# Gate rows stored from ScalarE, down sums moved, a row of its own for the last gate tile, head scaling on ScalarE, token blocks by column halves

## The chip, the core and the metric

The kernel runs on one core of one Trainium2 chip. A core has five engines that run side by side, each with an in-order queue of instructions: PE (TensorE, matrix products), DVE (VectorE), ACT (ScalarE), POOL (GpSimd) and SP (SyncE). DMA transfers are issued from the queues of SP, ACT and POOL and carried out by 16 DMA engines. An instruction that waits for something holds back all that stands behind it on its queue. Two memories on the chip matter here: SBUF, which holds tiles of 128 partitions, and PSUM, into which PE writes and which ACT and DVE read out.

The metric is the device time of one execution, in microseconds (us), the median of several runs.

## What is computed

One layer of a decoder trunk over 1024 tokens with 16 learned tokens ahead of them, D_MODEL 1024, in float32. A mixing block (a gated linear attention, "GLA", beside an "mLSTM") and then a convolutional feed-forward block. Cut to what the change touches:

```python
proj = h @ w_in + b_in.astype(h.dtype)
(g_q, g_k, g_v, g_r, g_lr, m_q, m_k, m_v, m_o, m_i, m_f, gate_a, gate_b) = jnp.split(proj, splits, axis=-1)
...
o_gla = from_chunks(head_rms(o_gla, gla_norm)) * jax.nn.silu(g_r)
...
o_ml = from_chunks(head_rms(o_ml, ml_norm.reshape(ML_H, 1, ML_DV))) * jax.nn.sigmoid(m_o)
y = jax.nn.sigmoid(gate_a) * (o_gla @ w_branch_gla) + jax.nn.sigmoid(gate_b) * (o_ml @ w_branch_ml)
return y @ w_out
```

`head_rms` scales each row of a head's output by its inverse root mean square. The feed-forward block is `(silu(gate) * up) @ w_down` with D_FF = 2816, after a causal convolution of width 3.

## The kernel before, in words

Channels lie on the partitions and tokens along the free dimension, in rows of 1040 (16 learned tokens and 1024). Every float32 operand of a product is split into a high part H, rounded for the matrix engine, and the rest L; a product is the sum of H*H, L*H and H*L, so three matmuls stand for one.

The stages, in order of time. Tiles are taken from pools; a tile with a tag shares its place with others of the same tag, and the first write to a reused place waits for the last use of the tile that had it.

*Heads* (to about 650 us). Four GLA heads (s = 0 to 3) and four mLSTM heads (s = 4 to 7). PE's main stream is the projections of the next head; the steps of the current head are a Python generator advanced between them. A head ends in `post` (L543): its output tiles `o(c)`, 128 tokens by 256 values for eight blocks, and `om` for the learned tokens, are scaled on POOL by a column of inverse norms (L548, L549), then transposed by PE (L558, tile "ot"; L564, "otm") and stored to DRAM (`osc`). The column itself is made on POOL as a power of -0.5 (L93). The three bare yields between put other work of PE's stream ahead of the transposes. After heads 3 to 6 `token_sums` (L458) makes sums and differences of token blocks on POOL, held behind `scaled`, the scaling of `om`, and stores them to DRAM (`tsc`).

*Gates* (about 650 to 1000 us). Thirty-two channel tiles of 128 are computed by `h @ w_in`: eight each of g_r, m_o, gate_a and gate_b. Six of gate_b (j = 0 to 3, 6 and 7) go one at a time through `merge_gate_b` (L450): 72 matmuls, three copies out of PSUM by ACT (L452) into a tile "gb" of tag "gst" (one buffer), and a store to DRAM (`gsc`, queue gscb) from SP. The tiles j = 0 to 2 run beside the last head, j = 3 as cover while the token blocks are loaded, and j = 6 and 7 after the pairs (END, L1137). The other 26 are taken in 13 pairs q (L1114 to L1135), each pair by a scheme of seven block products in place of eight: token halves and channel halves are summed and subtracted beforehand, which needs the token blocks T1 to T4 (`token_blocks`, L1059, tiles TH and TL from `tsc`) and the weight sums of `gate_weights` (L1008). `piece` (L960) is one of the two halves of a pair; its products go into the rows u0 and u1 (tiles gu0, gu1) by ACT (L984) and DVE (L977, L985, L986, L991, L992). The write of e2 (L985) is the first write of the pair into u1's second half; u1 has one buffer and u0 two.

`gate_finish` (L1078) ends a pair one step into the next: for pairs 0 to 7 it loads the head output, multiplies by the gate, and stores (`otd`); for pairs 8 to 12 it stores the raw rows u0 and u1 to `gsc` from POOL (L1082).

*Down sums.* `half_sums` (L1092) prepares the weights of the last product: two loads, four subtractions of [128 x 256] and two stores, all issued by POOL on one row. There are 22. Three follow each of the pairs 8 to 11 and two pair 12, four are made after the first merge product, and four in the loop over bm.

*Branch merge* (about 1000 to 1194 us). `load_o` (L1151) loads eight rows of a branch's output, splitting each (ACT makes ogH, DVE ogL). `prod3` (L1170) multiplies them by a branch weight, 72 matmuls of 342 columns into a PSUM tile of two buffers; for bg (GLA), j = 0 and 1 take the rows in the order in which they arrive. Each result is multiplied on DVE (L1203) by the sigmoid (ACT, L1200) of a gate_a row loaded by `merge_tile` (L1190). Rows yg4 to yg7 share places with the down sums of this stage (tags Y4 to Y7). Then come bm (mLSTM) with the gate_b rows sb, the output projection, and the feed-forward block to the end.

Order on each queue: the program is written in Python order, and a scheduler with priorities (`hp`) then places instructions, so what stands behind what on SP, ACT, DVE and POOL isn't the order of the source. `tc.issue_after(x)` asks that what follows on x's engine be placed behind x.

Of the kernel before, what the change touches and what calls it, by code (L numbers as in the profile page):

```python
# [17 lines left out]
P = 128  # L18
# [3 lines left out]
T = NM + SEQ  # L22
NK = D // P
NP = SEQ + 2
# [21 lines left out]
def hybrid_kernel(ctx, tc, x, meta, norm_mix, w_in, b_in, gla_w_gate, gla_b_gate, gla_norm,  # L46
                  ml_conv_w, ml_conv_b, ml_norm, w_branch_gla, w_branch_ml, w_out, norm_ffn,
                  ffn_w_up, ffn_conv_w, ffn_conv_b, ffn_w_down, norm_final, out):
    nc = tc.nc
# [9 lines left out]
    def hp(n):  # L59

        return tc.high_priority(offset=max(1, min(n, tc.cur_priority - floor[0])))
# [4 lines left out]
    wp = wctx.enter_context(tc.tile_pool(name="wp", bufs=3))  # L66
# [83 lines left out]
    def proj_cm(u, thirds, base, evac, bank=None):  # L150

        wH, wL = U.get(u, 2 if u > 2 else 0)
        for t0, n in thirds:
            pt = bank(t0) if bank else ps.tile([P, 512], F32, name=f"pj{u}_{t0}", tag="pj", bufs=3)
            i = 0
            for k in range(NK):
                for a, b in ((wH, xH), (wH, xL), (wL, xH)):
                    nc.tensor.matmul(pt[:, :n], a[:, k, :], b[:, k, base + t0:base + t0 + n],
                                     start=(i == 0), stop=(i == 3 * NK - 1))
                    i += 1  # L160
            with hp(PRI_E):
                evac(pt[:, :n], t0, n)
            yield
# [53 lines left out]
    TAIL, COVER, END = (0, 1, 2), (3,), (6, 7)  # L217
# [144 lines left out]
    for i in range(5, NC + 1):  # L362
        last, _ = norm_x(i)
# [6 lines left out]
    def cc(i):  # L370
        return col[:, i:i + 1]
# [34 lines left out]
    gsc = {g: dram.tile([NK, P, NP], F32, name=f"gsc{g}") for g in "ab"}  # L406
# [40 lines left out]
        heads[s]["v"] = vt  # L447
        yield from proj_v(uv[s], bB, vt)

    def merge_gate_b(j, bank=None):  # L450
        st = wp.tile([P, T], F32, name=f"gb{j}", tag="gst", bufs=1)
        yield from proj_cm(ugb[j], TH_POST, T0, lambda p, t0, n: nc.scalar.activation(  # L452
            st[:, t0:t0 + n], p, AF.Copy), bank)
        nc.sync.dma_start(gsc["b"][j], st[:, :NP])

    tsc = dram.tile([4, 4, P, 514], F32, name="tsc")

# [85 lines left out]
    def post(s, o, om, sc, ncols):  # L543

        h = s % 4
        g = "g" if s < 4 else "m"
        for c in range(NC):
            nc.gpsimd.tensor_scalar(o(c), o(c), sc[:, c + 1:c + 2], None, OP.mult)  # L548
        scaled = nc.gpsimd.tensor_scalar(om, om, sc[:2, 0:1], None, OP.mult)  # L549
        yield  # L550
        yield
        yield
        for j in range(2):
            of = hd.tile([P, T], F32, name=f"of{s}_{j}", tag="r", bufs=2)
            for gi in range(2):
                tp = ps.tile([P, 4, P], F32, name=f"ot{s}_{j}_{gi}", tag="s", bufs=3)
                for i in range(4):
                    nc.tensor.transpose(tp[:, i, :], o(4 * gi + i)[:, j * P:(j + 1) * P], ident)  # L558
# [5 lines left out]
            nc.tensor.transpose(tp[:, 0, :2], om[:, j * P:(j + 1) * P], ident[:2, :2])  # L564
# [351 lines left out]
    def advance():  # L916
        step(closing)
        while side and not step(side):
            pass
# [77 lines left out]
    gs = gs_ctx.enter_context(tc.tile_pool(name="gs", bufs=1, side="right", reuse_waits="tile"))  # L997
# [7 lines left out]
    NG = len(GATES) // 2  # L1005
# [47 lines left out]
    def weights_step(q):  # L1053
        if q < NG:
            next(wsteps[q])

    TB = {}

    def token_blocks():  # L1059
        for i in (0, 2, 1, 3):  # L1060
            h, l = TB[i] = [gs.tile([P, 4, 514], F32R, name=f"T{p}{i}", tag=f"T{p}{i}") for p in "HL"]
            nc.sync.dma_start(l.bitcast(F32), tsc[i].rearrange("k p c -> p k c"))
        for c in (slice(0, W0), slice(W0, 514)):
            for i in (0, 2, 1, 3):
                h, l = (t[:, :, c] for t in TB[i])
                nc.scalar.activation(h, l.bitcast(F32), AF.Copy)
                nc.vector.tensor_tensor(l, l.bitcast(F32), h.bitcast(F32), OP.subtract)
# [8 lines left out]
    gu = {}  # L1076

    def gate_finish(q):  # L1078
        for i, u in enumerate(gu.pop(q)):
            _, c, f, g, j = GATES[2 * q + i]  # L1080
            if f is None:
                nc.gpsimd.dma_start(gsc[g][j], u[:, :NP])  # L1082
                continue
            o = gs.tile([P, T], F32, name=f"go{q}_{i}", tag="o", bufs=2)
# [7 lines left out]
    def half_sums(pool, tag, bufs=1):  # L1092
        m, c = half.pop(0)
        t = pool.tile([P, T], F32, name=f"ts{m}{c}", tag=tag, bufs=bufs)[:, :D].rearrange("p (i n) -> p i n", i=4)
        for k in range(2):
            nc.gpsimd.dma_start(t[:, 2 * k:2 * k + 2], w_dn[P * (2 * m + k):P * (2 * m + k + 1), :].rearrange(  # L1096
                "p (i n) -> p i n", i=2)[:, :, 256 * c:256 * c + 256])
        for o, a, b in ((0, 1, 0), (1, 3, 1), (3, 3, 0), (2, 2, 3)):
            nc.gpsimd.tensor_tensor(t[:, o], t[:, a], t[:, b], OP.subtract)  # L1099
        for i in range(2):  # L1100
            nc.gpsimd.dma_start(tdn[i][m][:, :, 256 * c:256 * c + 256], t[:, 2 * i:2 * i + 2])
# [10 lines left out]
    u2 = wp.tile([P, T], F32, name="gu2", tag="gst", bufs=1)[:, :2 * W0].rearrange("p (a b) -> p a b", b=W0)  # L1112
    behind_ = None
    for q in range(NG):  # L1114
        gu[q] = [gs.tile([P, T], F32, name=f"gu{i}{q}", tag=f"u{i}", bufs=2 - i) for i in range(2)]
        for p in range(2):
            g = piece(psG, f"g{q}", p, gu[q], u2, WP[q], gate_block)
            next(g)
            if p == 1:
                weights_step(q + 1)  # L1120
            next(g)
            if p == 1:
                weights_step(q + 1)
            if behind_:
                next(behind_)
            if p == 0:
                weights_step(q)
                if q:
                    gate_finish(q - 1)
                weights_step(q + 1)  # L1130
            next(g)
            behind_ = g
        if q >= NK:
            for _ in range(3 if q < NG - 1 else 2):
                half_sums(gs, "o", 2)  # L1135
    next(behind_)
    for j in END:  # L1137
        ugb[j] = u_cm(w_in, O_GB + P * j, f"gb{j}")
    gate_finish(NG - 1)
    for j in END:  # L1140
        main(merge_gate_b(j, gate_bank(f"pe{j}")))
    gs_ctx.close()


# [2 lines left out]
    r2 = r2_ctx.enter_context(tc.tile_pool(name="r2", bufs=1, side="right", reuse_waits="tile"))  # L1147
# [34 lines left out]
    def th(t):  # L1182
        return t[:, :NP].rearrange("p (a b) -> p a b", a=3)
# [12 lines left out]
    for j in range(NK):  # L1196
        y = yg[j]
        if j < NK - 1:
            merge_tile(j + 1)
        nc.scalar.activation(y, y, AF.Sigmoid, bias=cc(C_GA + j))  # L1200
        pt = prod3(ubg[j], og, j < 2, f"bg{j}")
        with hp(PRI_E):
            nc.vector.tensor_tensor(th(y), pt, th(y), OP.mult)  # L1203
# [14 lines left out]
    for j in range(NK):  # L1218
# [6 lines left out]
        pt = prod3(ubm[j], om_, j < 1, f"bm{j}")  # L1225
# [237 lines left out]
    def po_bank(n, t, tag):  # L1463
        return psF.tile([P, 512], F32, name=f"po{n}_{t}", tag=tag)


    for i, tiles in enumerate(([1, 5, 2, 6, 0], [3, 7, 4, 8])):
        for n in range(4):
# [13 lines left out]
            for it, t in enumerate(rest):  # L1482
                pt = po_bank(n, t, ("V1", "X1")[it % 2])
# [19 lines left out]
    for q in range(NJ):  # L1503
        for p in range(2):
            g = up_piece(q, p)
# [239 lines left out]
    i = FIRST  # L1745
    while i < len(seq):
        r, ph, m = seq[i]
        k = i % NP2
# [52 lines left out]
```

## Time and profile before

| | us |
|---|---|
| median of 3 runs | 1978.6 |
| lowest and highest | 1977.29, 1978.92 |
| profiled execution | 1980.9 |
| its span, first to last instruction | 1979.2 |
| mean granted clock of PE | 0.977 |
| PE busy | 1880.7 |
| ACT busy | 827.7 |
| POOL busy | 461.3 |

How to read the rows below. A row of waits has the waiting engine, tile and line, what it waited for, and then the total, the number of waits and the longest. A row of the order of time has the start, the duration, engine, line and operation with output <- input; in brackets stands the idle time of the engine before it and what ended that. A row of windows has the stretch, its length, the busy time (with the number of instructions) of PE, PE's weight loads, DVE, ACT and POOL, and then PE's granted clock, the busy share of the DMA engines and GB/s. SPq is SP's queue, POOLq POOL's. Names of tiles are the program's, without buffer numbers.

### The profile page before, as it was taken

The numbers are of one execution on the slowest core, as the hardware profiler recorded it, in microseconds if no ns is written. First come the engines' busy times: TensorE is split into PE (matmuls) and PEld (weight loads), VectorE is DVE, ScalarE is ACT, GpSimd is POOL, SyncE is SP. The second block draws the span as 40 slices with busy tenths as digits, with TensorE's granted clock in tenths as the row PEclk, the third lists the DMA queues.
The fourth block names the chain that finished last, engine by engine and source line by source line (L and its number), as shares of the span: only waits on it lengthen the run. The fifth ranks groups of instructions, "written<-read, shape, count | busy, mean of one in ns | idle before, by whom it ended". The sixth has DMA issues, their size and how long they took to land. (4 is left out here: it accounts for less than half of the span.)

```text
span 1979.2 us, 32666 instructions
## 1 busy us (share of the span) xinstructions
PE 1880.7 (95%) x13377; PEld 1795.7 (91%) x13377; DVE 1196.8 (60%) x1775; ACT 827.7 (42%) x1297; POOL 461.3 (23%) x487
## 2 busy tenths in 40 slices
PE   8999999999999999965889999999999999999998
PEld 8999889899999999965889999999999999987776
DVE  6555636564442565644233344688787878886776
ACT  5354444544343433311142123554443434354563
POOL 3103303324353010177340120012222222200000
PEclk8999999999999999988889999999999999999999
DMA  5111011042322766666593353333334333378794
GB/s 162 33 36 57 22 56 53 16 131 72 96 76 80 182 164 157 159 187 180 166 343 105 106 188 101 129 119 111 102 108 133 107 107 107 113 270 308 282 375 157
DMA packets 220480, 270.02 MB, mean 136 GB/s; under 512 B 13422, under 2 KB 172672, under 8 KB 220331
## 3 DMA queue, kind: packets, MB, share of 16 engines
q1 hardware_dynamic: 205403, 220.95, 35.3%
q0 software_dynamic: 13088, 45.14, 7.5%
q8 instruction: 105, 1.72, 0.4%
q10 hardware_dynamic: 1840, 1.85, 0.3%
q14 instruction: 44, 0.36, 0.1%
HBM read 198.33 MB, written 69.57 MB: 135 GB/s over the span
## 5 line engine op out<-in xcount | busy, mean ns | idle before, releaser
L1361 POOL TENSOR_TENSOR SB<-SA,rg 128x512 f32<-128x512 f32 x20 | 32.0, 1598 | 234.9 <-issue 114.4
L1099 POOL TENSOR_TENSOR ts<-ts 128x256 f32<-128x256 f32 x88 | 74.5, 857 | 39.3 <-DMA ts<-in_ffn_w_down_dram 37.2
L201 PE MATMUL pv<-wH_mv,xH 128*128 128x256 f32 x256 | 75.5, 295 | 0.1
L201 PE MATMUL pv<-wH_gv,xH 128*128 128x256 f32 x256 | 75.3, 294 | 0.0
L957 PE MATMUL Yg<-xH,gHSB 128*128 128x258 f32 (+1 forms) x104 | 32.2, 309 | 43.7 <-DVE gu L985 43.7
L1448 PE MATMUL po<-wH_wo,yH 128*128 128x256 f32 x256 | 72.6, 284 | 0.1
L201 PE MATMUL pv<-wH_mv,xL 128*128 128x256 f32 x256 | 72.5, 283 | 0.0
L201 PE MATMUL pv<-wL_mv,xH 128*128 128x256 f32 x256 | 72.5, 283 | 0.0
L1448 PE MATMUL po<-wL_wo,yH 128*128 128x256 f32 x256 | 72.0, 282 | 0.3 <-DVE wL_wo L107 0.3
L201 PE MATMUL pv<-wH_gv,xL 128*128 128x256 f32 x256 | 72.0, 281 | 0.0
L201 PE MATMUL pv<-wL_gv,xH 128*128 128x256 f32 x256 | 72.0, 281 | 0.0
L1448 PE MATMUL po<-wH_wo,yL 128*128 128x256 f32 x256 | 71.7, 281 | 0.0
L1178 PE MATMUL bg<-ogH,wH_bg 128*128 128x342 f32 x192 | 62.7, 327 | 9.5 <-ACT gb L452 9.5
L1396 DVE SCALAR_TENSOR_TENSOR cv<-u,fc,cv 128x1024 f32<-128x1024 f32 x44 | 65.3, 1484 | 0.4
L1343 POOL TENSOR_TENSOR A<-u2raw,A 128x512 fp32r<-128x512 f32 x20 | 44.0, 2199 | 92.2 <-ACT A L1342 92.2
L1178 PE MATMUL bg<-ogL,wH_bg 128*128 128x342 f32 x192 | 62.7, 326 | 0.0
L1178 PE MATMUL bg<-ogH,wL_bg 128*128 128x342 f32 x192 | 62.5, 326 | 0.0
L957 PEld LDWEIGHTS Yg<-xH,gHSB 128*128 128x128 f32 x104 | 21.7, 209 | 44.7 <-DVE gu L985 44.7
L1096 POOL DMA_DIRECT2D ts<-in_ffn_w_down_dram x44 | 31.8, 728 | 128.9 <-DVE yM L1233 103.5
L675 POOL TENSOR_TENSOR pk<-pk,kT 128x256 f32<-128x256 f32 (+1 forms) x24 | 29.1, 1217 | 140.4 <-ACT pk L673 140.4
L1178 PE MATMUL bm<-omH,wH_bm 128*128 128x342 f32 x192 | 61.4, 320 | 0.0
L1178 PE MATMUL bm<-omH,wL_bm 128*128 128x342 f32 x192 | 61.3, 319 | 0.0
(749 smaller groups left out, 7566.6 us busy)
## 6 DMA issues: line engine op xcount, KB each, us to landing
gw<-in_w_in_dram SPq DMA_DIRECT2D x26, 512.0 KB
ts<-in_ffn_w_down_dram POOLq DMA_DIRECT2D x44, 256.0 KB, 4.4
tdn<-ts POOLq DMA_DIRECT2D x44, 256.0 KB, 2.7
rg<-in_ffn_w_up_dram SPq DMA_DIRECT2D x22, 512.0 KB
ru<-in_ffn_w_up_dram SPq DMA_DIRECT2D x22, 512.0 KB
adr<-s SPq DMA_DIRECT2D x40, 256.0 KB
rd<-in_ffn_w_down_dram SPq DMA_DIRECT2D x20, 512.0 KB
do<-tdn SPq DMA_DIRECT2D x18, 512.0 KB
```

The source lines that it names most:

```text
L201: nc.tensor.matmul(pt[:, :DV], a[:, k, t0:t0 + P], b[:, k % 4, :], start=(i == 0), stop=(i == 3 * NK - 1))
L675: eng.tensor_tensor(e, e, k, OP.mult)
L957: nc.tensor.matmul(out[:, :n], x[:, k, :], y[:, k, :], start=start and k == 0 and j == 0, stop=stop and k == 3 and j == 2, skip_group_chec ...
L1096: nc.gpsimd.dma_start(t[:, 2 * k:2 * k + 2], w_dn[P * (2 * m + k):P * (2 * m + k + 1), :].rearrange("p (i n) -> p i n", i=2)[:, :, 256 * c ...
L1099: nc.gpsimd.tensor_tensor(t[:, o], t[:, a], t[:, b], OP.subtract)
L1178: nc.tensor.matmul(pt[:, i, :n], a[:, k, :], b[k][:, t0:t0 + n], start=(k == 0 and j == 0), stop=(k == NK - 1 and j == 2))
L1343: eng.tensor_tensor(l, src, h.bitcast(F32), OP.subtract)
L1361: late.tensor_tensor(sb[:, 0:4], sa[:, 0:4], rg[:, 0:4], OP.subtract)
L1396: nc.vector.scalar_tensor_tensor(y, u[:, j:SEQ + j], fc[:, j, jj:jj + 1], y, OP.mult, OP.add)
L1448: nc.tensor.matmul(pt[:, :DV], a, b[:, k % 4, :], start=(k == 0 and i == 0), stop=(k == NK - 1 and i == len(terms) - 1))
```

## The change

It has five parts.

1. `gate_finish` issues its raw-row stores from ACT in place of POOL, and `merge_gate_b` issues its store from ACT in place of SP.
2. Pairs 8 to 11 are followed by two half sums in place of three. After the merge product bg1 three follow and after bg3 two, in place of four after bg0, written as held behind the merged product; the loop over bm takes the seven that are left (four before). The number of half sums is the same.
3. The last gate tile gb7 gets a row of tag "u0" (two buffers, free of gate pairs by then) in place of the single "gst".
4. `post` scales on ACT in place of POOL; after head 3 five yields stand before the transposes in place of three.
5. `token_blocks` takes the places of the tiles first and loads each by two column halves, all first halves ahead of the second; the first two rows go0 of tag "o" are taken between.

```diff
     def merge_gate_b(j, bank=None, st=None):
+        if st is None:
+            st = wp.tile([P, T], F32, name=f"gb{j}", tag="gst", bufs=1)
...
-        nc.sync.dma_start(gsc["b"][j], st[:, :NP])
+        nc.scalar.dma_start(gsc["b"][j], st[:, :NP])
...
         for c in range(NC):
-            nc.gpsimd.tensor_scalar(o(c), o(c), sc[:, c + 1:c + 2], None, OP.mult)
-        scaled = nc.gpsimd.tensor_scalar(om, om, sc[:2, 0:1], None, OP.mult)
-        yield
-        yield
-        yield
+            nc.scalar.activation(o(c), o(c), AF.Copy, scale=sc[:, c + 1:c + 2])
+        scaled = nc.scalar.activation(om, om, AF.Copy, scale=sc[:2, 0:1])
+        for _ in range(3 if s != 3 else 5):
+            yield
...
     def token_blocks():
         for i in (0, 2, 1, 3):
-            h, l = TB[i] = [gs.tile([P, 4, 514], F32R, name=f"T{p}{i}", tag=f"T{p}{i}") for p in "HL"]
-            nc.sync.dma_start(l.bitcast(F32), tsc[i].rearrange("k p c -> p k c"))
+            if i == 1:
+                places()
+            TB[i] = [gs.tile([P, 4, 514], F32R, name=f"T{p}{i}", tag=f"T{p}{i}") for p in "HL"]
         for c in (slice(0, W0), slice(W0, 514)):
+            for i in (0, 2, 1, 3):
+                nc.sync.dma_start(TB[i][1][:, :, c].bitcast(F32), tsc[i].rearrange("k p c -> p k c")[:, :, c])
...
+    def places():
+
+        for i in range(2):
+            go[0, i] = row(f"go0_{i}", "o", 2)
...
             if f is None:
-                nc.gpsimd.dma_start(gsc[g][j], u[:, :NP])
+                nc.scalar.dma_start(gsc[g][j], u[:, :NP])
                 continue
...
         if q >= NK:
-            for _ in range(3 if q < NG - 1 else 2):
+            for _ in range(2):
                 half_sums(gs, "o", 2)
...
-    for j in END:
-        main(merge_gate_b(j, gate_bank(f"pe{j}")))
+    for i, j in enumerate(END):
+        main(merge_gate_b(j, gate_bank(f"pe{j}"), row(f"gb{j}", "u0", 2) if i else None))
...
         with hp(PRI_E):
-            nc.vector.tensor_tensor(th(y), pt, th(y), OP.mult)
-        if j == 0:
-            for i in range(4, 8):
-                half_sums(r2, f"Y{i}")
+            merged = nc.vector.tensor_tensor(th(y), pt, th(y), OP.mult)
+        if j in (1, 3):
+            with tc.issue_after(merged.ins):
+                for i in (5, 6, 7) if j == 1 else (6, 7):
+                    half_sums(r2, f"Y{i}")
```

`row(name, tag, bufs)` is a [128 x 1040] tile of the gate stage's pool.

More of the change, by code (lines that the diff above doesn't have):

```diff
@@ L448, in value_proj, with merge_gate_b @@
         yield from proj_v(uv[s], bB, vt)
-    def merge_gate_b(j, bank=None):
-        st = wp.tile([P, T], F32, name=f"gb{j}", tag="gst", bufs=1)
+    def merge_gate_b(j, bank=None, st=None):
+        if st is None:
+            st = wp.tile([P, T], F32, name=f"gb{j}", tag="gst", bufs=1)
         yield from proj_cm(ugb[j], TH_POST, T0, lambda p, t0, n: nc.scalar.activation(
             st[:, t0:t0 + n], p, AF.Copy), bank)
-        nc.sync.dma_start(gsc["b"][j], st[:, :NP])
+        nc.scalar.dma_start(gsc["b"][j], st[:, :NP])
     tsc = dram.tile([4, 4, P, 514], F32, name="tsc")
@@ L1074, in gate_block, with row @@
         return [t[:, k0:k0 + 4, c0:c0 + n] for t in (xH, xL)]
-    gu = {}
+    gu, go = {}, {}
+    def row(name, tag, bufs=1):
+        return gs.tile([P, T], F32, name=name, tag=tag, bufs=bufs)
+    def places():
+        for i in range(2):
+            go[0, i] = row(f"go0_{i}", "o", 2)
     def gate_finish(q):
@@ L1081, in gate_finish @@
             if f is None:
-                nc.gpsimd.dma_start(gsc[g][j], u[:, :NP])
+                nc.scalar.dma_start(gsc[g][j], u[:, :NP])
                 continue
-            o = gs.tile([P, T], F32, name=f"go{q}_{i}", tag="o", bufs=2)
+            o = go[q, i] if q == 0 else row(f"go{q}_{i}", "o", 2)
             nc.gpsimd.dma_start(o[:, :NP], osc[g][j])
@@ L1114, in hybrid_kernel @@
     for q in range(NG):
-        gu[q] = [gs.tile([P, T], F32, name=f"gu{i}{q}", tag=f"u{i}", bufs=2 - i) for i in range(2)]
+        gu[q] = [row(f"gu{i}{q}", f"u{i}", 2 - i) for i in range(2)]
         for p in range(2):
```

## The prediction

> **What bounds the kernel now.** I read the page first, then the waits of PE, then the stretch in which the longest of them lie. One thing sets the end, PE:
>
> ```profile
> span 1979.2 us, 32666 instructions
> PE 1880.7 (95%) x13377; PEld 1795.7 (91%) x13377; DVE 1196.8 (60%) x1775; ACT 827.7 (42%) x1297; POOL 461.3 (23%) x487
> PE Yg L957 <- DVE gu L985: 43.7, 5, 15.6
> PE bg L1178 <- ACT gb L452: 9.5, 1, 9.5
> PE ot L558 <- POOL or L548: 5.0, 4, 2.3
> PE sc L626 <- POOL pk L675: 2.9, 3, 1.6
> PE sc L626 <- DVE pk L676: 2.7, 2, 1.7
> PE otm L564 <- POOL om L549: 0.6, 1, 0.6
> DVE gu L985 <- DMA gsca<-gu: 49.0, 4, 15.8
> ```
>
> PE has 98 us without work, and 43.7 of them are one line: the gate products wait for DVE's e2 write (L985). The last row says what DVE waits for: the landing of the store of a gate row. The same wait in order of time, with POOL, which issues that store:
>
> ```profile
> 852.82 0.41 DVE L992 TENSOR_TENSOR gu<-Zg,gu 128x256 f32<-128x256 f32 x1
> 873.38 0.42 DVE L985 TENSOR_TENSOR gu<-Yg,gu 128x256 f32<-128x256 f32 x1 [15.85 <-DMA gsca<-gu]
> 967.48 0.42 DVE L985 TENSOR_TENSOR gu<-Yg,gu 128x256 f32<-128x256 f32 x1 [10.60 <-DMA gsca<-gu]
> 864.61 0.81 POOL L1099 TENSOR_TENSOR ts<-ts 128x256 f32<-128x256 f32 x1
> 865.28 0.64 POOL L1082 DMA_DIRECT2D gsca<-gu  x1
> 957.22 1.20 POOL L1082 DMA_DIRECT2D gsca<-gu  x2
> ```
>
> The rows of pair 8 are whole at 853.2 (852.82 + 0.41). POOL, busy with half sums, issues the store of u1 only at 865.3 or 866.4, and it lands at 873.4. Tile u1 has one buffer, so the next pair's first write to it waits. Some 12 us are POOL's queue and 8 us travel. The first (15.85) and the last (10.60) of the four are shown.
>
> ```profile
> 780.00:840.00 60.00, 60.00 (x505) 60.00 (x504) 37.70 (x64) 22.27 (x33) 6.42 (x12) 1.00 0.67 163
> 855.00:980.00 125.00, 81.23 (x608) 80.21 (x607) 46.00 (x66) 18.86 (x30) 78.93 (x109) 0.82 0.59 176
> ```
>
> Two windows (busy time and count of PE, PEld, DVE, ACT, POOL, then PE's granted clock) price it. Undisturbed, 505 matmuls take 60 us, 0.1188 each. The 608 of the second window would take 72.2, with 0.4 more for eleven wider ones at its end; they took 125. The loss is **52 us**: 43.8 idle and about 8.6 of low clock after the idle times.
>
> [...]
>
> **1. Stores on ACT, two half sums per pair.** The eight gsca and two gscb stores are issued by ACT; they no longer queue behind half sums. Each new issue stands on ACT behind the copies of its pair and waits for the pair's last DVE write (L992). Behind it on ACT stand the next pair's copies from PSUM (L984), for which DVE and so PE wait; but those need products that come later anyway, and ACT is 15% busy there (18.86 of 125).
>
> The price of what remains: issue at 853.3, landing, and L985 takes 0.42. PE had waited 15.6 until 873.8, so it was ready at 858.2, and any L985 start up to 857.8 is free. No store from ACT's queue is in this trace. The nearest rows are the stores of the same 513 KB from SP's queue, whose landing the next copy into the same tile awaits:
>
> ```profile
> 648.50 0.32 SPq L454 DMA_DIRECT2D gscb<-gb  x1
> 653.71 0.46 ACT L452 ACTIVATE gb<-pc 128x342 f32<-128x342 f32 x1 [4.57 <-DMA gscb<-gb]
> 645.00:660.00 15.00, 15.00 (x97) 14.80 (x97) 4.52 (x8) 3.60 (x7) 0.54 (x1) 1.00 0.84 173
> 993.02 0.32 SPq L454 DMA_DIRECT2D gscb<-gb  x1
> 1001.27 0.80 ACT L452 ACTIVATE gb<-pe 128x342 f32<-128x342 f32 x2 [5.43 <-DMA gscb<-gb]
> 1005.00:1010.00 5.00, 0.14 (x1) 0.15 (x1) 2.69 (x3) 2.54 (x4) 3.29 (x5) 0.50 1.02 411
> gsca<-gu POOLq DMA_DIRECT2D x8, 513.0 KB, 8.1
> ```
>
> From issue to landing that is 5.2 us (653.71 - 648.50) at a share of the DMA engines of 0.84, and 8.3 (1001.27 - 993.02) where they are full (1.02 in the window from 1005). The stores from POOL took 8.1 (median, last row). The gate stage has a share of 0.59, so the first pair of rows is the nearest: landing at 858.5, 0.7 us late. With some ACT work in front of the issue (1 us) I take 1.25 for each of four pairs: **5 us remain**. Bounds: 0, and 4 x (853.3 + 8.3 - 857.8) = 15, with low clock up to 22. Gain 47, from 30 to 52.
>
> The half sums that leave the stage (14 become 10) are worked out under 3; inside the stage they free some 32 us of POOL (the time of four in the rows there), for which nobody then waits.
>
> **2. Scaling of heads on ACT.** 64 of L548 and eight of L549 leave POOL.
>
> ```profile
> L548 POOL TENSOR_SCALAR or<-or,rs3r 128x256 f32<-128x256 f32 x8 | 12.7, 1604 | 0.1
> L93 POOL TENSOR_TENSOR rs3r<-rs3v,mhalf 128x9 f32<-128x9 f32 x1 | 3.8, 3816 | 8.6 <-DVE rs3v L91 8.6
> L889 ACT ACTIVATE or<-op 128x256 f32<-128x256 f32 x32 | 12.2, 382 | 16.9 <-PE op L888 16.9
> ```
>
> The same shape takes ACT 0.38 us, so a head costs 8 x 0.38 + 0.4 (one for om) = 3.5 us of ACT instead of 7 to 13 of POOL. It removes PE's waits for L548 and L549, 5.0 + 0.6 = 5.6 us, all in head 3, where POOL's scaling takes 12.7. The two more yields for that head only put its transposes later. ACT has room: 8 x 3.5 = 28 on 828 of 1979. Behind each burst on ACT stand copies of the projection's sums; they come 3.5 us later at most, plus the wait for POOL's power (3.8 in head 3) if ACT gets there first. What hides that is the second PSUM buffer and PE's stream of projections. I take a gain of **5.6**; bounds: 11 (the waits of sc for pk, 2.9 + 2.7, go too) and a loss of 8.
>
> **3. End of the gates, branch merge.** Now the waits behind gb6 and gb7:
>
> ```profile
> 1007.46 1.06 ACT L1161 ACTIVATE ogH<-ogL 128x1026 fp32r<-128x1026 f32 x1 [2.47 <-DMA ogL<-otdg]
> 1009.86 0.65 PE L1178 MATMUL bg<-ogH,wH_bg 128*128 128x342 f32 x1 [9.49 <-ACT gb L452]
> 1024.20 1.23 DVE L1203 TENSOR_TENSOR yg<-bg,yg 128x1026 f32<-128x1026 f32 x1 [9.04 <-PE bg L1178]
> 989.91 2.85 POOL L1096 DMA_DIRECT2D ts<-in_ffn_w_down_dram  x4 [9.56 <-DMA gscb<-gu]
> 1021.16 0.68 POOL L1101 DMA_DIRECT2D tdn<-ts  x1 [0.30 <-POOL ts L1099]
> 980.53 2.38 SPq L1160 DMA_DIRECT2D ogL<-otdg  x4
> 1027.56 0.38 SPq L1160 DMA_DIRECT2D omL<-otdm  x1
> 1041.75 0.58 SPq L1160 DMA_DIRECT2D omL<-otdm  x1
> 1049.48 1.22 DVE L1203 TENSOR_TENSOR yg<-bg,yg 128x1026 f32<-128x1026 f32 x1
> ```
>
> gb7's copies waited for gb6's store; with its own row they don't, and the named 9.5 us go. But something else is late next. In the changed kernel's order SP issues, ahead of all eight ogL: a weight, the first sb (which waits for gb6's store), two omL (which wait for gb7's last matmul, 1009.86 - 9.49 = 1000.4) and the next weight (which waits for a split that needs gb7's weights released). So ogL leave at some 1004 and not from 980.53 on. The first ogH is then ready at 1011 to 1014, and bg0 takes its blocks in the pace of landings, 1.5 to 3.5 us each as the 2.47 shows. bg0 ends at 1025 to 1032 where it was 1024: a loss of 1 to 8, at best a gain of 2 (if loads land freely). I take 3.5.
>
> Then the five half sums that follow on POOL (Y5 to Y7 after bg1, Y6 and Y7 after bg3). Their hold by the merged product is not in the order of POOL's instructions; they begin when gb7's store frees the row, about 1006 to 1009. Before, four took 31.9 us (989.91 to 1021.84), five take 40. Behind the last stand yg7's load and six omL (14 us, 1027.56 to 1042.3), and the splits of omL stand ahead of the third merged product on DVE, which was at 1049.48 and would be at 1062 to 1070. PE needs that one's PSUM for bg4 at 1058 to 1064: 0 to 12, and I take **1**. Together **4.5 lost**. The seven in bm instead of four are 19 us more of POOL in a stage of 90 us; nothing waits for them before the down stage.
>
> **4. Token blocks by halves.**
>
> ```profile
> 649.54 10.30 SPq L1062 DMA_DIRECT2D TL<-tsc  x4
> 660.00:675.00 15.00, 12.18 (x93) 11.17 (x92) 10.67 (x10) 9.87 (x13) 0.00 (x0) 1.00 1.10 320
> PE Yg L957 <- DVE TL L1067: 0.9, 1, 0.9
> ```
>
> The four loads take 10.3 us on SP's queue since the third waits for a place; then PE starts the gates with idle time (2.8 in this window). With halves and the place taken before, it can go: gain **2.8**, bounds 0 and 2.8.
>
> **Sum:** 47 + 5.6 + 2.8 - 4.5 = 50.9. The profiled execution takes 1980.9 (span 1979.2 and 1.7 around it), 2.3 above the median of the runs, so 1930.0 there, and **1928** for the median of 1978.6.
>
> **Rivals.**
> - *A, the forecast*, 0.62: 1928, its own range 1918 to 1938.
> - *B, the merge stage pays much more*, 0.19: ogL land at 3.5 us each, 8 x 3.5 = 28 after 1011, so bg0 ends 15 late, and bg4's wait lies under that. For it speak full DMA engines (1.02) and the omL now ahead of them; against it the gaps of 1.5 seen too. 15 for 4.5: 1938.
> - *C, the change doesn't do what it says*, 0.12: the store's travel, not its place in a queue, is what DVE waits for. At 8.3 us from ACT as well, 15 to 22 remain for 5: 1938 to 1945, say 1941. For it: 8.1 of the 20 us from 853.2 to 873.4 were travel. Against it: 5.2 at a share of 0.84. [...]
> - *D, slower*, 0.04: ACT's bursts land on PE's path in every head. A burst is 3.5, with 3.8 before it for POOL's power: 7.3 x 8 = 58 more, 5.6 of gain gone: 1978.6 - 45.3 + 58 = 1991. It decides from 5.7 us a head on. Against it: ACT is 42% busy, and PE's waits in the heads name POOL and DVE.
> - The rest, 0.03: better than all that, down to 1914 (no remaining stall, heads 11, merge gains 2).
>
> B and C together would give 1951, so the range is **1915 to 1948**. A run tells about 0.2% (4 us) from no change: faster 0.94, same 0.02, slower 0.04.
>
> **What would show it.** 1: rows of L985 in pairs 9 to 12 with idle times below 3 us, clock 1.0 in the window after pair 8, and the last L992 some 47 us earlier. 2: no wait of ot for L548's successor, none larger of sc. 3: bg's first wait names ogH or ogL, and SP's ogL leave behind omL. 4: PE full between 660 and 675. Wrong would be: waits for gsca of over 4 us in each pair (C), or bg's waits above 15 us in sum (B).

## The result, and the profile after

| us | before | after |
|---|---|---|
| median | 1977.94 | 1960.26 |
| lowest to highest of 4 | 1975.61 to 1978.92 | 1959.70 to 1960.93 |
| profiled execution | 1980.9 | 1960.93 |

The ratio is 0.9912, with an interval of [0.9895, 0.993]: 17.7 us faster by the medians, 20.0 by the profiled executions. Forecast were 50.9: the sign came out, but 30.9 us of the gain, by the profiled executions, did not.

The span is 1959.2 us after, 1979.2 before. First the longest rows of the view of PE's waits (after; waiting tile, what it waited for, total, number, longest):

```profile
PE bg L1189 <- ACT ogH L1172: 15.8, 1, 15.8
PE bg L1189 <- DVE yg L1214: 11.2, 1, 11.2
PE po L1460 <- ACT hlo L1470: 6.3, 1, 6.3
PE Yg L957 <- DVE gu L985: 6.3, 5, 3.0
PE rtp L534 <- ACT of L560: 4.9, 1, 4.9
```

The 43.7 us of the gate rows have become 6.3. But bg, which waited 9.5 once, now waits 27.0 in two places, and two waits are new (rtp in head 3, po in the output projection).

Where in the execution that lies can be read without any idle time at all: the view of one line's instructions gives, for each group of matmuls, the start of the first and of the last. The last product of a stage is its end. After, then before:

```profile
L158 PE MATMUL pj<-xH,wH_gb x72: 313/318/508, 594.4 to 637.5; 128*128 128x342 f32 x72
L158 PE MATMUL pe<-xH,wH_gb x48: 313/318/430, 921.0 to 946.1; 128*128 128x342 f32 x48
L1189 PE MATMUL bg<-ogH,wL_bg x192: 313/320/487, 964.3 to 1070.9; 128*128 128x342 f32 x192
L1189 PE MATMUL bm<-omH,wL_bm x192: 313/319/325, 1071.4 to 1161.5; 128*128 128x342 f32 x192
L1460 PE MATMUL po<-wH_wo,yL x256: 277/282/415, 1161.9 to 1279.7; 128*128 128x256 f32 x128
```

```profile
L158 PE MATMUL pj<-xH,wH_gb x72: 313/318/509, 604.2 to 647.3; 128*128 128x342 f32 x72
L158 PE MATMUL pe<-xH,wH_gb x48: 313/318/425, 974.6 to 999.7; 128*128 128x342 f32 x48
L1178 PE MATMUL bg<-ogH,wL_bg x192: 312/320/488, 1010.6 to 1103.4; 128*128 128x342 f32 x192
L1178 PE MATMUL bm<-omH,wL_bm x192: 313/319/325, 1103.8 to 1194.0; 128*128 128x342 f32 x192
L1448 PE MATMUL po<-wH_wo,yL x256: 276/282/283, 1194.4 to 1299.9; 128*128 128x256 f32 x128
```

Differences of neighbouring ends give the length of each stage, beside what the prediction expected of it:

| stage (to the last ...) | before | after | gained | forecast |
|---|---|---|---|---|
| heads (gb2) | 647.3 | 637.5 | 9.8 | 5.6 |
| gates (gb7) | 352.4 | 308.6 | 43.8 | 49.8 |
| merge, GLA (bg7) | 103.7 | 124.8 | -21.1 | -4.5 |
| merge, mLSTM (bm7) | 90.6 | 90.6 | 0 | 0 |
| output projection (po) | 105.9 | 118.2 | -12.3 | 0 |

The feed-forward block differs by under 1 us. So 29 of the 31 us that are missing lie after the gates: 16.6 in the first merge product and 12.3 in the output projection. Both places follow, in order of time (after).

**The first merge product.** gb7's last matmul is over at 946.7.

```profile
946.76 0.81 SPq L1171 DMA_DIRECT2D omL<-otdm  x2
948.95 0.38 SPq L102 DMA_DIRECT2D wr_bg<-in_w_branch_gla_dram  x1
949.39 1.18 SPq L1203 DMA_DIRECT2D yg<-gsca  x1
950.74 9.68 SPq L1171 DMA_DIRECT2D ogL<-otdg  x8
960.11 1.15 ACT L1211 ACTIVATE yg<-yg,col 128x1026 f32<-128x1026 f32 x1 [5.89 <-DMA yg<-gsca]
961.39 1.06 ACT L1172 ACTIVATE ogH<-ogL 128x1026 fp32r<-128x1026 f32 x1
978.83 1.23 DVE L1214 TENSOR_TENSOR yg<-bg,yg 128x1026 f32<-128x1026 f32 x1 [1.62 <-PE bg L1189]
...
958.16 2.14 POOL L1107 DMA_DIRECT2D ts<-in_ffn_w_down_dram  x3 [50.14 <-DMA gscb<-gb]
998.90 0.68 POOL L1112 DMA_DIRECT2D tdn<-ts  x1 [0.30 <-POOL ts L1110]
1004.19 0.32 SPq L1203 DMA_DIRECT2D yg<-gsca  x1
1008.16 1.16 ACT L1211 ACTIVATE yg<-yg,col 128x1026 f32<-128x1026 f32 x1 [5.14 <-DMA yg<-gsca]
1009.23 1.04 ACT L106 ACTIVATE wH_bg<-wr_bg 128x1024 fp32r<-128x1024 f32 x1
1010.30 1.23 DVE L107 TENSOR_TENSOR wL_bg<-wr_bg,wH_bg 128x1024 fp32r<-128x1024 f32 x1 [19.70 <-ACT wH_bg L106]
1019.54 2.48 DVE L1173 TENSOR_TENSOR omL<-omL,omH 128x1026 fp32r<-128x1026 f32 x2 [1.94 <-ACT omH L1172]
1021.93 1.22 DVE L1214 TENSOR_TENSOR yg<-bg,yg 128x1026 f32<-128x1026 f32 x1
1023.30 0.63 PE L1189 MATMUL bg<-ogH,wH_bg 128*128 128x342 f32 x1 [11.25 <-DVE yg L1214]
```

Two losses. At bg0: SP has two omL, a weight and the first yg row ahead of the eight ogL; the omL wait for gb7's last matmul. The first split ogH runs on ACT at 961.39, behind the sigmoid of that yg row. The first merged product comes at 978.83, 32.1 after gb7's end; before, it came 23.8 after (1024.20 - 1000.4). That is 8.3. At bg4: POOL's half sums begin only when gb7's store has landed (958.16) and the last store leaves at 998.90. The row of yg7 shares its place, so its load leaves SP at 1004.19 and its sigmoid runs at 1008.16 on ACT, the high part of the next weight behind it at 1009.23, its low part on DVE at 1010.30, and then DVE splits six omL (the last two from 1019.54) before the merged product of bg2 at 1021.93. PE waits 11.2 for that one. The third merged product is 75.2 after gb7's end where it was 49.1 (1049.48 - 1000.4).

**The output projection.** PE's third new wait, in order of time (after):

```profile
1176.41 0.69 POOL L1112 DMA_DIRECT2D tdn<-ts  x1 [0.30 <-POOL ts L1110]
1179.06 0.34 SPq L1267 DMA_DIRECT2D h<-in_x_dram  x1
1179.56 0.68 SPq L102 DMA_DIRECT2D wr_wo<-in_w_out_dram  x1
1184.91 1.06 ACT L106 ACTIVATE wH_wo<-wr_wo 128x1024 fp32r<-128x1024 f32 x1 [6.18 <-DMA wr_wo<-in_w_out_dram]
1185.99 0.37 ACT L1470 ACTIVATE hlo<-po 2x256 f32<-2x256 f32 x1
```

The seventh half sum of the mLSTM stage uses the row Y6, and its last store leaves POOL at 1176.41. A row h of the output projection shares that place: its load stands on SP until 1179.06, the weights wr_wo stand behind it on SP, the split wH_wo waits for them on ACT (6.18), and hlo, which empties the PSUM bank that PE wants, stands behind that split. Four queues pass one late store on.

### The profile page after: what moved, and what is told of

The parts are those of the page before. It is cut to its first block, busy times and chain, and to the rows that moved or that the text cites. A ratio compares the mean times of both kernels' runs of the same rounds, so it can differ in the third digit from the quotient of the medians.

```text
span 1959.2 us, 32654 instructions
## 1 busy us (share of the span) xinstructions
PE 1876.5 (96%) x13377; PEld 1791.5 (91%) x13377; DVE 1187.0 (61%) x1775; ACT 857.1 (44%) x1369; POOL 372.8 (19%) x405
## 3 DMA queue, kind: packets, MB, share of 16 engines
q8 instruction: 105, 1.72, 0.4%
## 5 line engine op out<-in xcount | busy, mean ns | idle before, releaser
L1189 PE MATMUL bg<-ogH,wH_bg 128*128 128x342 f32 x192 | 63.3, 331 | 27.0 <-ACT ogH L1172 15.8
L1373 POOL TENSOR_TENSOR SB<-SA,rg 128x512 f32<-128x512 f32 x20 | 32.1, 1605 | 235.9 <-issue 114.1
L1189 PEld LDWEIGHTS bg<-ogH,wH_bg 128*128 128x128 f32 x192 | 37.7, 197 | 27.5 <-ACT ogH L1172 16.1
L1189 PE MATMUL bm<-omL,wH_bm 128*128 128x342 f32 x192 | 61.2, 319 | 0.0
```

Of the source, the lines that this page charges most:

```text
L1189: nc.tensor.matmul(pt[:, i, :n], a[:, k, :], b[k][:, t0:t0 + n], start=(k == 0 and j == 0), stop=(k == NK - 1 and j == 2))
L1373: late.tensor_tensor(sb[:, 0:4], sa[:, 0:4], rg[:, 0:4], OP.subtract)
```

## The experiments

The kernels ran on three chips, whose medians of the kernel before were 1977.8 (first four), 1972.2 (next four) and 1976.3 (last three), so ratios are compared; the changed kernel's is 0.9912. The stage lengths come from the same rows as above, in each kernel's profile, so each is that of one execution. Stages with the same code differ between executions: the gates take 300.4 in e6 and 309.1 in e10, whose edits differ only behind them, and the stages of the kernel before take 352.4 (gates) and 103.7 (GLA merge) in its profile, 344.0 and 99.7 in e8, which changes the heads alone. A difference in the gates of under 9 us, or in the merge of under 4, shows nothing by itself.

| | ratio to before, interval | median | gates | GLA merge | output proj. |
|---|---|---|---|---|---|
| e1 | 0.9831 [0.9811, 0.9852] | 1944.7 | 304.6 | 110.5 | 115.7 |
| e2 | 0.9859 [0.9835, 0.9883] | 1952.5 | 311.5 | 125.3 | 107.6 |
| e3 | 0.9900 [0.9885, 0.9915] | 1958.1 | 306.6 | 122.9 | 116.4 |
| e4 | 0.9812 [0.9787, 0.9838] | 1940.8 | 303.7 | 111.0 | 107.0 |
| e5 | 0.9856 [0.9829, 0.9882] | 1942.9 | 303.8 | 109.1 | 117.6 |
| e6 | 0.9817 [0.9796, 0.9839] | 1934.4 | 300.4 | 111.6 | 107.2 |
| e7 | 0.9880 [0.9855, 0.9905] | 1946.1 | 319.3 | 105.7 | 106.2 |
| e8 | 0.9966 [0.9947, 0.9985] | 1963.0 | 344.0 | 99.7 | 107.3 |
| e9 | 0.9794 [0.9772, 0.9815] | 1936.4 | 310.3 | 107.6 | 108.4 |
| e10 | 0.9781 [0.9766, 0.9796] | 1932.2 | 309.1 | 105.0 | 107.6 |
| e11 | 0.9770 [0.9740, 0.9801] | 1931.3 | 307.6 | 99.4 | 110.5 |

**e1: gb7 shares its row again.** The changed kernel without part 3.

```diff
-        main(merge_gate_b(j, gate_bank(f"pe{j}"), row(f"gb{j}", "u0", 2) if i else None))
+        main(merge_gate_b(j, gate_bank(f"pe{j}"), None))
```

> The changed kernel with part 3 alone undone: gb7 goes back to the one row of tag gst; its copies wait for gb6's store again. Theory (the own row is what the merge stage pays for: it moves the eight ogL loads behind omL and weights on SP, and it holds POOL's first half sum of the merge stage until gb7's store has landed): bg0's merged product about 24 us after gb7's last matmul (32 in the changed kernel, 24 before), POOL's first load of that stage some 25 us earlier than 958, PE's 11.2 us wait in bg gone, time 1940 (1935 to 1945). Rival (the five half sums and DVE's order of omL splits make the wait in bg, wherever POOL starts): bg0 is 8 earlier but the wait in bg grows by as much, time 1958 to 1961. Second rival (the own row is a gain of its 9.5 us, the rest lies elsewhere): slower, 1968.

The GLA merge is 14.3 us shorter, and the time at the upper end of the expected range. The view of its order of time:

```profile
922.95 3.58 SPq L1171 DMA_DIRECT2D ogL<-otdg  x5
925.45 1.44 POOL L1107 DMA_DIRECT2D ts<-in_ffn_w_down_dram  x2 [16.22 <-DMA gscb<-gu]
```

Five ogL leave 19 us before gb7's last product (942.2), and POOL's half sums start before it too (925.45), because the row that they wait for is released by the stores of pair 12 and not by gb7's. So the own row costs more than the 9.5 us that it takes away.

**e2: one half sum moved from the mLSTM merge into the gates.** Six where the changed kernel has seven.

```diff
-            for _ in range(2):
+            for _ in range(3 if q == NK else 2):
```

> The changed kernel with one half sum moved: three after pair 8, so that the loop over bm has six and not seven, and none lands on the row Y6 that h7's load needs next. Theory (the seventh half sum holds h7's load on SP until 1179, and the weights of the output projection stand behind it): PE's wait for hlo of 6.3 us goes, the output projection takes 106 us as before instead of 118, time 1948 (1946 to 1951). Rival (the output projection is slowed by the load of POOL, ACT and DMA at the end of bm): six for seven is worth 2 us, 1958. A cost in the gates, if POOL is at its limit there: L985's waits above 8 us in sum.

The wait for hlo is gone and the output projection is 10.6 shorter, back near before's 105.9. The seventh half sum is the cause of the third loss: in every experiment without it the output projection takes 106.2 to 110.5, in every one with it 115.7 or more. The gates are 2.9 longer, with 8.4 us of waits for L985 instead of 6.3, which is within what one execution differs from another. The median is 1.5 above the expected range.

**e3: DVE's splits of omL behind the merged product of bg2.** This takes the splits out of the way of the merged product for which PE waited.

```diff
+        prods.append(merged)
...
-    om_ = load_o("m", r1b, "R")
+    with tc.issue_after(prods[2].ins):
+        om_ = load_o("m", r1b, "R")
```

> The changed kernel with DVE's eight splits of omL queued behind the third merged product (bg2) and nothing else moved by hand; the half sums and yg7's load stay as late as they are. Theory (PE's 11.2 us wait in bg is DVE's order: the merged product of bg2 stands behind omL's splits, which wait for omL's loads behind yg7's): the wait goes, bg ends some 13 us earlier with the clock, time 1947 (1944 to 1951). Rival (yg7's late load itself sets it, through ACT, where wH_bg4 stands behind yg7's sigmoid): a wait for wL_bg of 5 to 11 us takes its place, time 1955 to 1961.

Only 1.9 us, no more than executions differ. bg still waits 9.6 us for yg, 8.8 of it at once. DVE in order of time:

```profile
1010.22 1.22 DVE L1215 TENSOR_TENSOR yg<-bg,yg 128x1026 f32<-128x1026 f32 x1
1021.52 9.18 DVE L1173 TENSOR_TENSOR omL<-omL,omH 128x1026 fp32r<-128x1026 f32 x8
1030.62 1.22 DVE L1215 TENSOR_TENSOR yg<-bg,yg 128x1026 f32<-128x1026 f32 x1
```

bg2's product is now early (1010.22), but all eight splits come in one piece before the next, and PE waits for that one. The wait moved by one product. As I had stated it, the theory fell: the place behind bg2's product only hands the wait on. The rival's time came (1958.1), but not the wait for wL_bg that it named. The place behind bg4's product is tried in e5 and e10.

**e4: the stores alone.** The kernel before, with one line of the change: the raw gate rows stored from ACT.

```diff
-                nc.gpsimd.dma_start(gsc[g][j], u[:, :NP])
+                nc.scalar.dma_start(gsc[g][j], u[:, :NP])
```

> The kernel before with one edit: the raw gate rows of pairs 8 to 12 are stored from ACT, not POOL; three half sums per pair stay, and all other parts of the change are left out. Theory (the place of the store in POOL's queue was the 44 to 47 us): L985's waits from 43.7 to 5 to 8 us, last gate matmul 42 to 47 earlier, and since the merge stage keeps its order, most of it arrives: 1936 (1930 to 1945). Rival (three half sums per pair can't be had without the stalls: POOL lags some 15 us behind and the merge stage's half sums, yg7 and omL come later): 1945 to 1955. Second rival (fewer half sums, not the queue, gave the gain): 1970 or more.

One edit gives 37 us by the medians, twice what the whole change gives. The gate stage is 48.7 shorter than in the profile before, and 40.3 shorter than in that of e8, whose gates have the code before. L985 waits 2.8 us in all, the longest 1.9, and the granted clock stays at 1.00 (window from 850 to 950 us). The GLA merge is 7.3 longer than before's: bg's waits are 10.9 (for gb) and 4.0 (for yg), and nothing waits for hlo.

**e5: the two orders by hand, everything else as changed.** On SP the loads of omL and sb go behind the last ogL; on DVE the splits of omL go behind the fifth merged product.

```diff
...
-    om_ = load_o("m", r1b, "R")
+    with tc.issue_after(loads[-1].ins), tc.issue_after(prods[4].ins):
+        om_ = load_o("m", r1b, "R")
...
-        nc.sync.dma_start(sb, gsc["b"][j])
+        with tc.issue_after(loads[NK - 1].ins):
+            nc.sync.dma_start(sb, gsc["b"][j])
```

> The changed kernel, gb7's own row and the five late half sums kept, but two orders set by hand: on SP the omL and sb loads behind the last ogL, on DVE the eight splits of omL behind the merged product of bg4 (the third run put them behind bg2's, and the wait went to bg5). Theory (the half sums that start late are the root; the orders on SP and DVE hand the delay on): bg0 up to 8 us earlier, but wH_bg4 still stands on ACT behind yg7's sigmoid, so bg4 can't start before about 65 us after gb7's last matmul; the stretch from there to bg's end falls from 125 to 111 to 114, time 1947 to 1950. Rival (the orders are the whole cost and the late half sums are harmless): the stretch falls to 104 as before the change, time 1940. Second rival (the wait only moves to another product again): 120 or more, 1956.

The GLA merge is 15.7 shorter with gb7's own row kept; the waits for yg fall from 11.2 to 2.0, the one for ogH from 15.8 to 11.2. The 109.1 lies between the theory's 111 to 114 and the rival's 104. And POOL's half sums are still late: their first load starts at 950.57, after 44.55 us of waiting for gb7's store. So the late half sums alone cost little (2.0 us of waits here); together with the splits ahead of bg2's product on DVE they cost more. The queue orders carry some 16 of the 21 us.

**e6: e1 and e2 together.**

> The changed kernel with gb7 back on the shared row and one half sum moved from bm to behind pair 8 (runs one and two together). If the two costs are separate, they add: 1944.7 - 8 to 10 = 1935 to 1937, bg's stretch 110, the output projection 107. If the eleventh half sum in the gates delays the merge stage's as much as it gains, 1943 or more with bg's stretch above 115.

The GLA merge (111.6) is close to that of e1, the output projection (107.2) that of e2: the two costs are separate. In the ratio it is 0.95% below the change (19 us), where the two stages say 14.3 + 10.6 = 24.9; its interval is 8 us wide. By the ratio the sum did not come in full: 1935 to 1937 on the first chip would be 0.979.

**e7: the change without parts 2 and 3.** Half sums and gb7 as before; stores, scaling and token blocks as changed.

```diff
...
-        if j in (1, 3):
-            with tc.issue_after(merged.ins):
-                for i in (5, 6, 7) if j == 1 else (6, 7):
-                    half_sums(r2, f"Y{i}")
+        if j == 0:
+            for i in range(4, 8):
+                half_sums(r2, f"Y{i}")
```

> The changed kernel without parts 2 and 3: stores on ACT, head scaling on ACT, token blocks by halves; half sums and gb7's row as before. Theory (parts 2 and 3 are what gave the gain back): 1940.8 of the run with the stores alone, less 6 for the heads and 3 for the token blocks: 1932 (1928 to 1936); bg's stretch 110, the output projection 107. Rival (parts 4 and 5 are worth nothing on top, the stages before the gates differ from run to run by as much): 1940.

A miss: 14 us above the 1932 expected, and 22 by the ratios, since this chip is the fastest of the three. By the ratios it is also 13 slower than e4. A wait that no other kernel has stands in the gates, 15.7 us of the last gate tiles (pe) for ACT's copy L453. POOL, SP and ACT in order of time:

```profile
940.38 0.68 POOL L1112 DMA_DIRECT2D tdn<-ts  x1 [0.30 <-POOL ts L1110]
943.06 2.70 SPq L1171 DMA_DIRECT2D ogL<-otdg  x5
949.41 1.06 ACT L1172 ACTIVATE ogH<-ogL 128x1026 fp32r<-128x1026 f32 x1 [19.50 <-DMA ogL<-otdg]
```

With three half sums a pair POOL lags; the first ogL leaves SP 2.7 us after a half sum's store at 940.38, which by these times is what it waits for. The split ogH stands on ACT ahead of gb6's last copy (951.32), so the gates' own products wait for a load of the next stage. e6 and e7 differ in the places of the half sums alone, and e6 is 11.7 us faster by the medians. The prediction gave part 2 no worth in the gates; beside the other parts it has one. e4 has three half sums a pair too and no such wait; it lacks parts 4 and 5 and the store of gb from ACT, and which of these makes the difference was not tried.

**e8: the scaling alone.** The kernel before with part 4 of the change.

> The kernel before with part 4 alone: the scaling of the heads on ACT and five yields after head 3. My step: the waits of ot and otm go and nothing new comes, 5.6 us: 1972 (1967 to 1976), last gate_b matmul of the heads' stage some 6 us earlier. Rival (ACT's bursts cost as much as they save): 1977 to 1982. If more than 8 us are gained, POOL's other work in the heads (pk) was held up by the scaling as well.

0.34% of 1972.2 is 6.7 us, 3 to 10 by the interval, for the 5.6 expected. But it isn't the expected 5.6. PE's waits for the scaled tiles are gone, and in their place, as in the changed kernel, stands the 4.9 of rtp. Windows of the second part of the GLA heads, in e8 and in e4 (which scales on POOL):

```profile
160.00:325.00 165.00, 162.60 (x1135) 151.94 (x1134) 100.16 (x166) 87.93 (x162) 23.51 (x24) 1.00 0.17 51
```

```profile
160.00:325.00 165.00, 159.76 (x1119) 149.36 (x1118) 97.67 (x162) 79.52 (x142) 41.65 (x42) 1.00 0.16 48
```

At the same clock PE is busy 2.8 us more of this stretch, with 18 us of POOL's work gone. The last GLA value projection starts at 316.1 in e8 and 320.1 in e4, the last matmul of gb2 at 637.8 and 643.6: 4.0 of the 5.8 us come before head 3's scaling. What is seen of waits there are those of sc for pk on POOL (2.9 before, 0.5 in the changed kernel); the rest of the 4.0 isn't assigned. That the gates and the GLA merge of e8 are 8.4 and 4.0 shorter than in the profile before is not shown to come from the scaling.

**e9: e5 and e2 together; e10: e6 with the splits of omL behind the fifth merged product.**

> The fifth run's orders with the second run's six half sums in bm; gb7's own row kept. If the three costs are separate (order on SP, order on DVE, h7's load), bg's stretch stays at 109 and the output projection falls from 118 to 107: ratio to the kernel before 0.980 (0.977 to 0.983). If the eleventh half sum in the gates delays the late half sums further, yg7's sigmoid holds wH_bg4 and bg's stretch grows to 114 or more: 0.983 to 0.986.

> The sixth run (gb7 on the shared row, six half sums in bm) with the splits of omL behind bg4's merged product on DVE. Theory (the 4.9 us wait for the merged product there is the same order on DVE): it goes, bg's stretch falls from 111.6 to 105 to 107, ratio 0.979 (0.977 to 0.982). Rival (yg7's sigmoid on ACT holds bg4 anyway): a wait of 3 to 5 for wL_bg in its place, ratio unchanged at 0.982.

In these two stages both come out as the sum of their parts: GLA merge 107.6 and 105.0, output projection 108.4 and 107.6. In e10 one order on DVE is all that differs from e6, and its 4.9 us wait for yg is gone. Two ways around the losses, with gb7's own row or without, end within each other's intervals.

**e11: the rows of the merge first.** e9, with two weights (bg3, bg4) and the first yg row behind the last ogL on SP, and the sigmoids of yg behind the last ogH on ACT.

```diff
-        nc.sync.dma_start(raw, src)
+        with tc.issue_after(loads[NK - 1].ins) if name in ("bg3", "bg4") else nullcontext():
+            nc.sync.dma_start(raw, src)
...
-    merge_tile(0)
     og = load_o("g", r2, "O")
+    with tc.issue_after(loads[-1].ins):
+        merge_tile(0)
...
-        nc.scalar.activation(y, y, AF.Sigmoid, bias=cc(C_GA + j))
+        with tc.issue_after(highs[NK - 1].ins):
+            nc.scalar.activation(y, y, AF.Sigmoid, bias=cc(C_GA + j))
```

> The ninth run, and the loads of ogL first of all in the merge stage: the weights of bg3 and bg4 and yg0 behind them on SP, yg0's sigmoid behind the ogH on ACT; gb7's own row is kept. Theory (what is left of the start is the place of the ogL in SP's queue): PE's first wait of bg falls from 11 to below 5, bg0's merged product comes 22 to 26 us after gb7's last matmul where it is 28 in the fifth run, bg's stretch 100 to 105, ratio 0.976 (0.973 to 0.979). Rival (it is the DMA engines, full there whatever the order): first wait 9 or more, ratio as in the ninth run.

SP in order of time (lines are a few lower in this kernel):

```profile
928.52 24.23 SPq L1175 DMA_DIRECT2D ogL<-otdg  x8
```

The ogL now leave from 928.52 on, seven of the eight before gb7's last matmul (which starts at 946.0), bg's first wait is 2.8 us, and the GLA merge takes 99.4: 25 less than in the changed kernel and as long as the 99.7 of e8 with the order before. POOL's half sums start late here too (953.12). It is 45 us faster than before (1976.3 to 1931.3) and, by the ratios, 28 faster than the change. By their intervals it and e10 can't be told apart.

## Why the prediction was wrong, and where it was right

**Step 1, the stores: right, and near in size.** Remaining waits of L985 behind pairs 8 to 11 were put at 5 us for four; the rows below, in order of time, show the longest of them, and 6.3 less the 1.06 of the first pair (in the last fence of this section) leaves 5.2. That the sum fits is in part luck: it was 1.25 for each, and one is 2.97. e4, the edit by itself, shortens the stage by 40 to 49, depending on which profile of these gates it is held against, for the 47 predicted. Rival C, that travel and not POOL's queue is the wait, is out.

```profile
863.58 0.33 ACTq L1093 DMA_DIRECT2D gsca<-gu  x1
871.62 0.42 DVE L985 TENSOR_TENSOR gu<-Yg,gu 128x256 f32<-128x256 f32 x1 [3.50 <-DMA gsca<-gu]
872.10 0.58 PE L957 MATMUL Yg<-xH,gHSB 128*128 128x258 f32 x1 [2.97 <-DVE gu L985]
```

and the window behind it:

```profile
873.00:877.00 4.00, 4.00 (x21) 4.00 (x21) 1.76 (x2) 0.00 (x0) 4.00 (x6) 0.50 0.60 153
```

What was off is one landing: 8.0 us from the issue at 863.58, close to the upper bound (8.3) and not the 5.2 chosen. The DMA engines were full there (a share of 1.12 from 863.6 to 871.6), so the row of the 8.3 was the nearest one, and not that of 5.2, chosen by the stage's mean share of 0.59. After PE's wait of 2.97 the clock is 0.50 for four us, where the 5 us of the prediction had no low clock in them; that is some 2 us. The low clock that its bound adds to 15 to make 22, some 7 us for four waits of 3.8, is a term that no run shows: what the changed kernel showed is these 2, behind one wait. In e2 and e10 the clock fell to 0.50 after shorter waits as well, of 1.72 to 1.94 (the last section has a row).

**Step 2, the scaling: right in size by luck, wrong in place and price.** The 5.6 of waits in head 3 went, and 4.9 came back as rtp's wait for ACT (L560); most of what was gained came from elsewhere. The price of the scaling on ACT was taken from a row of another form, too low:

```profile
L549 ACT ACTIVATE or<-or,rs3r 128x256 f32<-128x256 f32 x8 | 3.3, 496 | 3.7 <-POOL rs3r L93 3.7
```

496 ns and not 382, so a head costs 4.5 us of ACT and not 3.5. The gain came from the GLA heads before 325 us (e8). In the stage table the heads gain 9.8; e4, whose heads are before's own, ends them at 643.6, so 6.1 are the change's and 3.7 go with before's profiled execution, whose clock was 0.98 from 160 to 325 us where e4 had 1.00.

**Step 3, the merge: the step that failed first.** "4.5 lost" was made of 3.5 at bg0, from a range of 1 to 8, and of 1 at bg4, from 0 to 12. They measured 8.3 and 12.8 (21.1 less 8.3). The mechanism was told right, queue by queue; each value was taken below the middle of its own range, the second near its kind end, and the result is just above both unkind ends. At bg0, the first split ogH was put at 10.6 to 13.6 us after gb7's end (1011 to 1014 less 1000.4) and was ready 15.8 after: its load travels while the DMA engines are full (a share of 0.99 between 946.7 and 962.5). The sigmoid ahead of it on ACT adds little at most, since seven of the eight splits wait for their own loads (5.7 us in all). At bg4, the third merged product was put at 62 to 70 us after gb7's end (1062 to 1070 less 1000.4) and came 75.2 after. A link was left out of that chain: the sigmoid of yg7 also holds back the next weight's high part on ACT, for which DVE waits 19.7 us before it comes to the splits of omL. No run moves that sigmoid alone. Rival B gave this outcome 0.19 with 15 lost at bg0; the loss is larger and most of it is at bg4. B's own sign, waits of bg above 15 us in sum, is there with 27.0.

**The sentence that failed outright** is the last of step 3: the seven half sums in the mLSTM stage are "19 us more of POOL in a stage of 90 us; nothing waits for them before the down stage". It asked who reads the sums, not who takes their rows next. h does, and through SP and ACT that cost 12.3 (e2 gives 10.6 of them back). No rival had it, and with the merge's loss it carries the time out of the range.

**Step 4, the token blocks: nothing gained.** The idle times of 2.8 are there in the kernel after as well, under other names. Before, four waits for the blocks make 2.7, the longest 1.11. PE and ACT in order of time, after:

```profile
657.88 0.39 PE L957 MATMUL Xg<-TH,gHSB 128*128 128x258 f32 x1 [1.90 <-DVE gu L977]
664.51 1.06 ACT L1069 ACTIVATE TH<-TL 128x1024 fp32r<-128x1024 f32 x1 [3.47 <-DMA TL<-tsc]
666.35 0.39 PE L957 MATMUL Yg<-xH,gHSB 128*128 128x258 f32 x1 [1.06 <-DVE gu L985]
```

The 2.7 us of waits for the blocks are now 3.0 us of waits for DVE's rows. Both kernels split the blocks in eight pieces, on ACT and then on DVE, and behind these splits stand the pair's copies: ACT's last piece waits 3.47 for its load, the copy out of PSUM (L984) runs behind it at 665.47, DVE's L985 waits for that copy, and PE for L985. The blocks still come late; the wait for them has moved behind ACT and DVE. The bound of 0 was the right end; no run takes this part alone.

**The sum.** Of 30.9 us that the profiled execution falls short, 16.6 are the GLA merge, 12.3 the output projection and 6.0 the gates (2.8 the token blocks, 2 low clock, the rest not assigned), less 4.2 that the heads gave above the forecast; that leaves 0.2 for all else. Most of the 4.2 is the 3.7 of before's profiled execution (step 2).

## What to carry to other kernels

When work is moved to a later stage, ask of each buffer that it holds who takes that place next, and follow that taker through its queue: here one store late on POOL held a load on SP, the weights behind it, a split on ACT and at last PE. Where a term is the end of such a chain, and other work is queued on its links, take the middle or the unkind end of its range unless every link's queue has been read: both terms here came out above their ranges. And run the parts of a change one by one: one line of the first of the five was worth twice the whole.

## What the runs showed of the hardware that was not expected

In the changed kernel the granted clock fell to 0.50 behind a wait of PE of 2.97 us. It also did behind shorter ones: 1.94 and 1.72 in e2, 1.76 in e10. Yet it stayed at 1.00 behind 2.52 in e1 and 2.28 in e11. One of each, e2 and then e1, with a window behind it:

```profile
849.55 0.39 PE L957 MATMUL Yg<-xH,gHSB 128*128 128x258 f32 x1 [1.94 <-DVE gu L985]
851.60:853.60 2.00, 2.00 (x11) 2.00 (x10) 0.32 (x1) 0.00 (x0) 1.90 (x4) 0.50 0.54 159
869.61 0.39 PE L957 MATMUL Yg<-xH,gHSB 128*128 128x258 f32 x1 [2.52 <-DVE gu L985]
871.70:873.70 2.00, 2.00 (x19) 2.00 (x19) 0.89 (x3) 0.00 (x0) 2.00 (x3) 1.00 0.37 56
```

So in these runs, between 1.7 and 3 us, the length of a wait alone doesn't tell whether the clock falls; what does, no run here shows. It may be one reason why the same gates differ between executions: e10 (309.1) has three such falls in the gates, e6 (300.4), whose longest wait for L985 is 1.51, has none.

Moving ten stores to another engine's queue saved 40 to 49 us of a stage (e4). A transfer could still be as long: one took 8.0 us in the changed kernel, where the median from POOL's queue was 8.1 before. But the issue of pair 8's store had stood for some 12 us behind half sums on POOL's queue (853.2 to 865.3 before), and such waits were the gain.
